# One pool of six PSUM banks, in-place operands counted as inputs, and another order of attention steps in a two-layer encoder trunk

## The chip, the cores and the metric

The kernel runs on one core of a Trainium2 chip. Its engines are TensorE (PE, with weight loads as PEld), VectorE (DVE), ScalarE (ACT), GpSimd (POOL) and SyncE (SP, which issues the DMAs). The metric is device microseconds of one launch. The kernel before has a median of 954.72 us in three runs (953.11 to 955.43).

## The reference

256 tokens of width 1024 pass two layers. Each layer is a half-step SwiGLU block, a mixer, and a second half-step SwiGLU block (width 2816); every block adds to the residual. The mixer of layer 0 is recurrent, that of layer 1 is differential attention whose keys and values are made from the residual between the layers:

```python
x = x + 0.5 * swiglu(rmsnorm(x, g1), wg, wu, wd)
# layer 0
proj = h @ w_in;  gate, rec = split(proj)
rec = causal_depthwise_conv(rec, conv_w, conv_b)          # 4 taps
r, i = sigmoid(rec @ w_a + b_a), sigmoid(rec @ w_x + b_x)  # blocks of 128
a = exp(-8 * r * softplus(-lam))
h_t = a_t * h_{t-1} + sqrt(1 - a_t**2) * i_t * rec_t
x = x + (gelu(gate) * h) @ w_out
# layer 1, 8 heads with two query/key halves of 64 each, chunk-causal mask
q, k = rope(rmsnorm(h @ w_q)), rope(rmsnorm(hkv @ w_k));  v = hkv @ w_v
p = softmax(mask(q @ k.T));  attn = p[0] - lam * p[1]
x = x + (rmsnorm(attn @ v) * (1 - lam0)) @ w_o
x = x + 0.5 * swiglu(rmsnorm(x, g2), wg, wu, wd)
```

Inputs, weights and output are float32.

## The kernel before, in words

Activations lie transposed in SBUF, as eight tiles of 128 features by 256 tokens. Every float32 product is made from three fp32r products: operands are split into a rounded part (`hi`) and a rest (`lo`), and `hi*hi + hi*lo + lo*hi` is summed in PSUM (`mm2` writes the two halves of the activation side by side, 512 columns and then 256; `mm3` issues three matmuls into one sum). Weights come from one array `wts`, laid out by the host in the order in which the steps use them, in pieces of 1 MB; SP loads a piece into `raw`, ACT casts eight 128x128 blocks into `whi` and DVE subtracts to get `wlo` (`split`). So each weight costs PE, ACT and DVE work.

Four stages of feed-forward (`ffn`) surround the two mixers. The recurrent stage (`recurrent`) follows `REC_STEPS`: R0 to R7 are projections of eight feature blocks, each followed by its four-tap convolution on DVE (`taps`: the first tap on ACT, then three in-place `scalar_tensor_tensor`, then a split); L0 to L7 the gate products of those blocks; G the gate projections; D the decay; E the GELU; M the merge; O the output projection. The attention stage follows `ATT_STEPS`: Q, K and V are projections (0: heads 0 to 3, 1: heads 4 to 7; each makes one tile for each of two blocks of 128 tokens, 48 matmuls of 512 columns in all); after Q and K come the norm, the rotation and a transpose (`qk_post`); S0 and S3 are the softmaxes of the first token block for four heads, S1, S2, S4 and S5 those of the second for two heads (`softmax`: scores, on DVE a mask and a maximum, on ACT one exponential for each head and half with a sum, on DVE the combination, on PE a transpose); A0 to A6 multiply with the values and normalise (`av`: its output is squared and scaled on ACT, then transposed on PE); O is the output projection. The letters behind a step say from which PSUM group its tiles come.

PSUM has eight banks. Before, `MB = 4` of them serve tiles named `mm`, `SB = 2` tiles named `sc`, `AB = 2` the tiles `aux` (transposes, norms, the products of A, L0, L1 and L7 of the recurrent stage). A step with tag `m` takes the next free `mm` bank, one with `s` the next free `sc` bank.

The order on each engine is not the order of the code. All calls are recorded (`Recorder.add`, which finds the earlier operations each one depends on from the memory it reads and writes), and `Recorder.plan` lays them out on the five engines: it takes at each step the operation that can start first, with a preference for the one with the longest chain behind it (`tails`), from a duration that `cost` gives. The recorded order of TensorE operations is itself a chain in `tails`, so it acts as their priority. `emit` then issues everything, which is why all instructions carry line 375. In the queues each engine works strictly in that order. `add` distinguishes, for two operations on one engine, a true read after write (`op.raw`: the second waits for the result) from mere order (the second starts when the first has been issued). The inputs are taken as all operands that are not the very object of the output, so an operation that overwrites an operand in place, such as a tap `xcj = rp*w + xcj`, is not counted as reading it.

Of the kernel before, what the change touches and what calls it, by code (L numbers as in the profile page):

```python
# [11 lines left out]
F32 = mybir.dt.float32  # L12
# [6 lines left out]
P = 128  # L19
D = 1024  # L20
KD = 8
T = 256
# [6 lines left out]
SUBLN_EPS = 1e-5  # L29
FG = 2  # L30
REC_STEPS = (
    "W R0s W R1s R2s R3s R4m L0a L1a R5s R6m W L2s L3s R7s G0m D0 L4m L5m L6m L7a G1s E0 E1 G2m E2 "
    "G3s M0 E3 D1 H4a M1 M2 E4 M3 H6m O0 M4 E5 M5 W W O1 E6 M6 E7 O2 O3 M7"
).split()
ATT_STEPS = (
    "Q0mm K0ss K1mm S0mm S1mm Q1ss V0mm A0 S2ms S3ms A2 V1sm S4mm S5mm O0 A4 O1 O2 A6 O3 O4 O5"
).split()
REC_OUT = "0m 1m 23m 45m 67s"
ATT_OUT = "0m 1m 23m 45m 67s"
# [24 lines left out]
DA = 1  # L64
SA = 2
DM = (8, 8, 8, 7)
MB = 4
SB = 2
AB = 2

B_GU = NF * KD * 2
# [24 lines left out]
def is_ap(v):  # L96
    return hasattr(v, "tensor") and hasattr(v, "ap")


def width(v):  # L100
    n = 1
    for _, c in v.ap[1:]:
        n *= c
    return n


def region(v):
    size = mybir.dt.size(v.dtype)
    row = v.ap[0][0]
    lo = v.offset % row if row else v.offset  # L110
    hi = lo + sum(s * (c - 1) for s, c in v.ap[1:]) + 1
    if v.space == bass.MemoryType.PSUM:
        return 0, 1 << 20
    return lo * size, hi * size


def cost(op):
    k, out = op.k, op.outs[0] if op.outs else None
    ins = [v for v in list(op.a) + list(k.values()) if is_ap(v) and not any(v is o for o in op.outs)]
    psum = [v for v in ins if v.space == bass.MemoryType.PSUM]  # L120
    n = width(out) if out is not None else 1
    if op.eng == "tensor":
        if op.fn == "transpose":
            return 109, 220
        m = width(k["rhs"])
        if k["rhs"].dtype == BF16:
            return m / 2.4 + 3, m / 2.4 + 175
        if k["rhs"].dtype == F32R:
            return 0.4508 * m + 2.6, 0.4508 * m + 165
        p = 4 * m / 2.4 + 3 if m > 8 else 222  # L130
        if k["lhsT"].ap[0][1] <= HD:
            p /= 2
        return p, p + 170
    if op.eng == "scalar":
        if op.fn == "preload_act_table":
            return 1294, 1283
        scaled = is_ap(k.get("scale")) or is_ap(k.get("bias"))
        p = n / 1.2 + ((65 + 20 * scaled) if psum else (100 + 85 * scaled))
        lat = n / 1.2 + (172 if psum else 195 + 90 * scaled)
        return (p + 93, lat + 200) if len(op.outs) > 1 else (p, lat)  # L140
    if op.eng == "vector":
        if op.fn in ("reduce_sum", "reduce_max"):
            n = width(ins[0])
        if op.fn == "tensor_copy":
            return n / 1.92 + 67, n / 1.92 + 155
        if op.fn == "memset":
            return n / 0.96 + 10, n / 0.96 + 50
        if op.fn == "tensor_tensor_scan":
            return n * 2 / 0.96 + 55, n * 2 / 0.96 + 140
        rate = 0.96  # L150
        if op.fn == "tensor_scalar" and not psum:
            rate = 1.92
        scalar = op.fn in ("tensor_scalar", "scalar_tensor_tensor") and len(ins) > (1 if op.fn == "tensor_scalar" else 2)
        return n / rate + (125 if scalar else 68), n / rate + (210 if scalar else 153)
    if op.eng == "gpsimd":
        if op.fn == "memset":
            return 30, 100
        if k.get("op") == ALU.pow:
            return 300 + 170 * n, 340 + 170 * n
        return 120 + 2.14 * n, 160 + 2.14 * n  # L160
    return 420, 0


class Recorder:
# [16 lines left out]
    def add(self, eng, fn, a, k):  # L181
        op = Op()
        op.i, op.eng, op.fn, op.a, op.k = len(self.ops), eng, fn, a, k
        op.deps, op.users, op.tiles, op.raw = set(), [], set(), set()
        op.outs = [v for v in ([k["out"]] if "out" in k else list(a[:1])) + [k.get("accum_out")] if is_ap(v)]
        ins = [v for v in list(a) + list(k.values()) if is_ap(v) and not any(v is o for o in op.outs)]
        op.pitch, op.lat = cost(op)
        op.port = False
        op.narrow = eng == "tensor" and fn == "matmul" and k["lhsT"].ap[0][1] <= HD
        if eng in ("vector", "gpsimd"):  # L190
            big = [v for v in ins if v.space != bass.MemoryType.PSUM and width(v) > 1]
            one = fn in ("tensor_scalar", "tensor_copy")
            op.port = len(big) >= (1 if one else 2) and k.get("op") != ALU.pow and fn != "memset"
        for v, w in [(v, False) for v in ins] + [(v, True) for v in op.outs]:
            if v.space == bass.MemoryType.DRAM:
                continue
            name = v.tensor.name
            lo, hi = region(v)
            if name not in self.hist:
                self.hist[name] = []  # L200
                t = v.tensor
                self.tiles[name] = dict(tag=t.tag, bufs=t.tag_meta.bufs, acc=set(), k=self.seen.setdefault(t.tag, 0))
                self.seen[t.tag] += 1
            for j, l, h, ww in self.hist[name]:
                if (w or ww) and l < hi and lo < h:
                    self.depend(op, j)
                    if ww and not w:
                        op.raw.add(j)
            if w:
                self.hist[name] = [x for x in self.hist[name] if not (lo <= x[1] and x[2] <= hi)]  # L210
            self.hist[name].append((op.i, lo, hi, w))
            self.tiles[name]["acc"].add(op.i)
            op.tiles.add(name)
        key = "load" if eng == "sync" and k["out"].space != bass.MemoryType.DRAM else self.key
        if key is not None:
            self.depend(op, self.last.get(key))
            self.last[key] = op.i
        self.ops.append(op)
        return op
# [193 lines left out]
def trunk(ctx: ExitStack, tc, plan, xT, wts, vec, rows, eye, out):  # L413
    nc = Recorder(tc.nc)

    def pool(name, bufs, **kw):
        return Pool(nc, ctx.enter_context(tc.tile_pool(name=name, bufs=bufs, **kw)), bufs, plan and plan[1])
# [5 lines left out]
    wsp = pool("wsp", GB)  # L423
    psm = pool("psm", MB, space=bass.MemoryType.PSUM)
    psa = pool("psa", AB, space=bass.MemoryType.PSUM)
# [62 lines left out]
    def mm2(ps, b, xs, start, stop):  # L488
        wh, wl = wblk(b)
        nc.tensor.matmul(out=ps, lhsT=wh, rhs=xs, start=start, stop=False)  # L490
        nc.tensor.matmul(out=ps[:, 0, :], lhsT=wl, rhs=xs[:, 0, :], start=False, stop=stop)
# [16 lines left out]
    def bank(shape, tag="m"):  # L508
        if tag == "a":
            return psa.tile(shape, F32, name="aux")  # L510
        if tag == "s":
            return psm.tile(shape, F32, name="sc", bufs=SB)
        return psm.tile(shape, F32, name="mm")

    def split_scaled(dst, src, gain):
# [89 lines left out]
    def ffn(i, xs, rb_fn, after, hook=None):  # L605
        rb = None
        hs = []
        o = O_FFN[i]
# [15 lines left out]

        pss = {}
        for f in range(NF):
            pss[f] = ps = [bank([P, 2, T], "mms"[f % 3]) for _ in range(2)]
            if f < FG:
                if f == FG - 1:
                    for k in range(KD):  # L630
                        for ff in range(FG):
                            for j in range(2):
                                mm2(pss[ff][j], o + k * 2 * FG + ff * 2 + j, xs[k], k == 0, k == KD - 1)
            else:
                for k in range(KD):
                    for j in range(2):
                        mm2(ps[j], o + f * 16 + k * 2 + j, xs[k], k == 0, k == KD - 1)
            if f < FG - 1:
                continue
            if f == FG - 1:  # L640
                _, rb = rb_fn()
                for ff in range(FG):
                    finish(ff, pss.pop(ff))
            else:
                finish(f, pss.pop(f))
            if hook and f == 5:
                hook()
        o += B_GU
        for d in range(KD):
            if d < DM[i]:  # L650
                ps = psm.tile([P, 2, T], F32, name="mm")
# [6 lines left out]
            else:  # L658
                ps = psm.tile([P, T], F32, name="mm")
# [89 lines left out]

    xs_mix = new_xs()  # L750
    ffn(0, xs, lambda: rstd("f10"), prep(xs_mix, V_MIX[0]), small)

    def recurrent(xs, rb_fn, after):
# [110 lines left out]
    def after_l0(d):  # L864
        pr1(d)
        split_scaled(xkv[d], x[d], vt[:, V_KV + d:V_KV + d + 1])

    ffn(1, xs_f20, lambda: rstd("f20"), after_l0)

    kvrt = {}  # L870
# [5 lines left out]

    xs_q = new_xs()
    ffn(2, xs_f11, rs_l1, prep(xs_q, V_MIX[1]))

    def attention(xs, rt_q, rt_kv, after):  # L880
# [277 lines left out]
```

## Time and profile before

| | us |
|---|---|
| median of three runs | 954.72 |
| the profiled execution | 954.38 |
| its span, from first to last instruction | 952.6 |
| PE busy | 937.7 |
| DVE busy | 727.9 |
| ACT busy | 582.1 |

Mean granted TensorE clock: 0.995 of full speed. The trace gives for each engine the start and duration of its instructions and, where it was idle before one, what ended the wait. A matmul's duration contains its drain, so durations of neighbours overlap; what one costs is the distance from start to start. In a row of a timeline, x4 stands for four equal instructions in a row, and the bracket at the end holds the idle time before the first of them and what ended it.

### The profile page before, as it was taken

To read this page: it belongs to the slowest core of one execution; us is meant where nothing else is said; L and a number is where in the kernel's file an instruction comes from. 1 tells how busy PE (TensorE), PEld (TensorE's weight loads), DVE (VectorE), ACT (ScalarE), POOL (GpSimd) and SP (SyncE) were. 2 spreads that over 40 slices of the span, in tenths; PEclk is the share of its full clock that TensorE was granted. 3 is DMA by queue.
4 is the path that set the end of the run, shared out by engine and by line. 5 is a ranking of instruction groups with operands and counts; after the bars stand their busy time and mean duration, and the time that the engine had idled before them with its cause. 6 is when DMAs were issued, how large, how long until landed. Compare 5 with 4: busy or idle time off the path is not lost. (4 is left out here: it accounts for less than half of the span.)

```text
span 952.6 us, 14673 instructions
## 1 busy us (share of the span) xinstructions
PE 937.7 (98%) x5586; PEld 828.9 (87%) x5586; DVE 727.9 (76%) x1226; ACT 582.1 (61%) x1039; POOL 36.7 (4%) x42
## 2 busy tenths in 40 slices
PE   8999999999999999999999999999988999999998
PEld 7888888899998888888888888888776988888887
DVE  7998877689988878866788787667985588788751
ACT  7665565569966565656565656545577766656541
POOL 0400000000000000000000000003110000000000
PEclk9999999999999999999999999999999999999999
DMA  8655556543365555555555555555523245555540
GB/s 321 244 206 182 194 199 221 183 172 131 122 231 182 195 201 177 183 208 184 178 182 206 187 182 195 198 177 177 175 91 132 95 175 194 201 177 186 213 161 17
DMA packets 25991, 172.33 MB, mean 181 GB/s; under 512 B 3136, under 2 KB 4288, under 8 KB 5568
## 3 DMA queue, kind: packets, MB, share of 16 engines
q1 hardware_dynamic: 25920, 171.39, 51.5%
q8 instruction: 44, 0.72, 0.3%
q14 instruction: 27, 0.22, 0.1%
HBM read 170.33 MB, written 1.05 MB: 180 GB/s over the span
## 5 line engine op out<-in xcount | busy, mean ns | idle before, releaser
L375 DVE TENSOR_TENSOR wlo<-raw,whi 128x1024 fp32r<-128x1024 f32 (+1 forms) x321 | 390.7, 1221 | 132.4 <-ACT whi L375 131.2
L375 ACT CAST whi<-raw 128x1024 fp32r<-128x1024 f32 (+1 forms) x321 | 335.8, 1047 | 199.3 <-PE mm L375 140.5
L375 PE MATMUL mm<-xs,whi 128*128 128x512 f32 (+1 forms) x1056 | 352.4, 382 | 1.3 <-DVE xs L375 0.9
L375 PE MATMUL mm<-b,whi 128*128 128x512 f32 (+1 forms) x918 | 282.7, 365 | 1.8 <-ACT w L375 1.7
L375 PE MATMUL mm<-xs,wlo 128*128 128x256 f32 x1008 | 281.3, 280 | 0.1
L375 PEld LDWEIGHTS mm<-xs,whi 128*128 128x128 f32 x1056 | 194.5, 188 | 41.5 <-DVE xs L375 1.4
L375 PE MATMUL mm<-b,wlo 128*128 128x256 f32 x800 | 225.0, 282 | 0.0
L375 PEld LDWEIGHTS mm<-b,whi 128*128 128x128 f32 x918 | 165.7, 189 | 30.8 <-ACT w L375 2.3
L375 PEld LDWEIGHTS mm<-xs,wlo 128*128 128x128 f32 x1008 | 190.3, 189 | 0.8 <-DVE wlo L375 0.5
L375 PE MATMUL sc<-xs,whi 128*128 128x512 f32 (+1 forms) x576 | 182.1, 371 | 0.1
L375 PEld LDWEIGHTS mm<-b,wlo 128*128 128x128 f32 x800 | 152.1, 190 | 0.0
L375 PE MATMUL sc<-xs,wlo 128*128 128x256 f32 x512 | 145.1, 283 | 0.0
L375 PEld LDWEIGHTS sc<-xs,whi 128*128 128x128 f32 x576 | 105.0, 191 | 18.7 <-ACT w L375 0.3
L375 ACT ACTIVATE w<-mm 128x256 f32<-128x256 f32 x151 | 57.7, 384 | 77.5 <-PE mm L375 76.3
L375 PEld LDWEIGHTS sc<-xs,wlo 128*128 128x128 f32 x512 | 97.6, 191 | 0.1
L375 DVE TENSOR_TENSOR w<-mm,w 128x256 f32<-128x256 f32 x120 | 49.8, 420 | 17.0 <-ACT w L375 16.9
L375 DVE TENSOR_TENSOR w<-w,rb 128x512 f32<-128x512 f32 x88 | 60.1, 689 | 0.7
L375 DVE TENSOR_TENSOR w<-w,w 128x256 f32<-128x256 f32 (+2 forms) x104 | 45.2, 439 | 0.1
L375 ACT ACTIVATE w<-w 128x256 f32<-128x256 f32 x88 | 36.4, 418 | 9.8 <-DVE w L375 7.4
L375 ACT ACTIVATE w<-sc 128x256 f32<-128x256 f32 x56 | 21.5, 384 | 31.7 <-PE sc L375 31.7
L375 ACT CAST b<-w 128x256 fp32r<-128x256 f32 x88 | 35.4, 406 | 5.6 <-DVE w L375 5.5
L375 DVE TENSOR_TENSOR b<-w,b 128x256 fp32r<-128x256 f32 x88 | 36.5, 418 | 1.9 <-ACT b L375 1.9
(160 smaller groups left out, 686.2 us busy)
## 6 DMA issues: line engine op xcount, KB each, us to landing
raw<-wts SPq DMA_DIRECT2D x159, 1024.0 KB, 4.8
raw<-wts SPq DMA_DIRECT2D x3, 512.0 KB, 6.8
outT<-xa SPq DMA_DIRECT2D x8, 128.0 KB, 2.0
xa<-xT SPq DMA_DIRECT2D x3, 256.0 KB, 6.0
raw<-wts SPq DMA_DIRECT2D x2, 256.0 KB, 3.7
rw<-rows SPq DMA_DIRECT2D x1, 320.0 KB, 5.9
xa<-xT SPq DMA_DIRECT2D x1, 260.0 KB, 3.6
ident<-eye SPq DMA_DIRECT2D x1, 64.0 KB, 9.1
```

The costliest lines, as they stand in the source:

```text
L375: getattr(getattr(self.nc, op.eng), op.fn)(*op.a, **op.k)
```

## The change

Four things change. The two groups `mm` (4 banks) and `sc` (2) become one group of six. `cost` and `add` take their inputs from a new helper, `sources`, which counts an operand that is also the output. The letters `s` vanish from the tables, and `ATT_STEPS` has another order: both K projections directly after Q0 (K1 first), S1 before Q1 and S0 after it, S2 and S3 around the first A2 of the list, A6 before O2. `ATT_STEPS` also orders the weights on the host, so the pieces of K1 and K0 change places.

```diff
 ATT_STEPS = (
-    "Q0mm K0ss K1mm S0mm S1mm Q1ss V0mm A0 S2ms S3ms A2 V1sm S4mm S5mm O0 A4 O1 O2 A6 O3 O4 O5"
+    "Q0mm K1mm K0mm S1mm Q1mm S0mm V0mm A0 S2mm A2 S3mm V1mm S4mm S5mm O0 A4 O1 A6 O2 O3 O4 O5"
 ).split()
...
-MB = 4
-SB = 2
+MB = 6
...
+def sources(a, k):
+    vals = list(a if "out" in k else a[1:]) + [v for n, v in k.items() if n not in ("out", "accum_out")]
+    return [v for v in vals if is_ap(v)]
...
 def cost(op):
     k, out = op.k, op.outs[0] if op.outs else None
-    ins = [v for v in list(op.a) + list(k.values()) if is_ap(v) and not any(v is o for o in op.outs)]
+    ins = sources(op.a, k)
...
-        ins = [v for v in list(a) + list(k.values()) if is_ap(v) and not any(v is o for o in op.outs)]
+        ins = sources(a, k)
         op.pitch, op.lat = cost(op)
...
-        if tag == "s":
-            return psm.tile(shape, F32, name="sc", bufs=SB)
...
-            pss[f] = ps = [bank([P, 2, T], "mms"[f % 3]) for _ in range(2)]
+            pss[f] = ps = [bank([P, 2, T], "m") for _ in range(2)]
```

Since the planner decides, the diff does not show what moves. Three places do. In all of them a number behind a name counts the tiles in recorded order.

PE in attention, from the last matmul of Q1 to the start of V0, before: `mm_1466` and `mm_1467` are the two halves of S0, `mm_1476` and `mm_1477` those of S1, `sc_1526` the second half of S2, `mm_1507` and `mm_1508` the two token blocks of V0.

```order
L375 MATMUL sc_1486<-whi_1490,xs_0_1012 128x512
L375 MATMUL mm_1466<-b_0_1383,b_0_1381 128x128
L375 MATMUL mm_1467<-b_0_1383,b_0_1381 128x128
...
L375 MATMUL mm_1476<-b_0_1383,b_0_1381 128x256
L375 MATMUL mm_1477<-b_0_1383,b_0_1381 128x256
...
L375 MATMUL sc_1526<-b_0_1383,b_0_1381 128x256 x2
L375 MATMUL mm_1507<-whi_1493,xk_644 128x512
...
L375 MATMUL mm_1508<-whi_1493,xk_644 128x512
```

The same place after the change: here `mm_1466` and `mm_1467` are S1, `mm_1498` and `mm_1499` S0, and `aux_1492` is the transpose of the first token block of Q1.

```order
L379 MATMUL mm_1477<-whi_1481,xs_0_1012 128x512
L379 MATMUL mm_1466<-b_0_1383,b_0_1381 128x256
L379 MATMUL mm_1467<-b_0_1383,b_0_1381 128x256
...
L379 MATMUL mm_1498<-b_0_1383,b_0_1381 128x128
L379 MATMUL mm_1499<-b_0_1383,b_0_1381 128x128
...
L379 MATMUL mm_1507<-whi_1484,xk_644 128x512
...
L379 MATMUL mm_1507<-whi_1512,xk_644 128x512
L379 MATMUL aux_1492<-ident_79,w_2_1490 128x128 x4
```

S1 stands before S0, the second half of S2 is gone from here, and V0 starts in one bank alone: nineteen matmuls of its first token block come before the second block takes a bank. By the planner's list of banks V0 took those of S0 before; now its first block takes that of Q1's first block, and its second block that of S1's first half.

ACT between V0 and the transposes inside V1, before: `w_3_1529` and `w_1_1530` are the exponentials of S2, `w_4_1539` and `w_5_1540` those of S3, and the rows with `aux_1519` square (with `oss`) and scale (with `ofr`) the output of A0.

```order
L375 ACTIVATE w_3_1529,sm_1528<-mm_1525,mx_1527,facq_0_1387 128x256 x2
L375 ACTIVATE w_1_1530,sm_1528<-sc_1526,mx_1527,facq_0_1387 128x256 x2
L375 ACTIVATE w_2_1522,oss_1520<-aux_1519,ra_1472 128x128
...
L375 ACTIVATE w_4_1539,sm_1538<-mm_1535,mx_1537,facq_0_1388 128x128 x4
L375 ACTIVATE w_5_1540,sm_1538<-sc_1536,mx_1537,facq_0_1388 128x128 x4
L375 ACTIVATE w_2_1522<-aux_1519,ofr_1523 128x128 x4
```

The same place after the change; S3's exponentials are now `w_5_1545` and `w_2_1546`.

```order
L379 ACTIVATE w_3_1529,sm_1528<-mm_1525,mx_1527,facq_0_1387 128x256
L379 ACTIVATE w_4_1522,oss_1520<-aux_1519,ra_1504 128x128
...
L379 ACTIVATE w_3_1529,sm_1528<-mm_1525,mx_1527,facq_0_1387 128x256
L379 ACTIVATE w_0_1530,sm_1528<-mm_1526,mx_1527,facq_0_1387 128x256 x2
L379 ACTIVATE w_5_1545,sm_1544<-mm_1541,mx_1543,facq_0_1388 128x128 x4
L379 ACTIVATE w_2_1546,sm_1544<-mm_1542,mx_1543,facq_0_1388 128x128 x4
L379 ACTIVATE w_4_1522<-aux_1519,ofr_1523 128x128 x4
```

The same sixteen instructions stand ahead of the four that scale A0's output; only the squares have moved up between those of S2.

PE in the recurrent stage, at L6 (`mm_572`), L7 (`aux_574`) and the gate projection behind them (`sc_576`, now `mm_576`), before:

```order
L375 MATMUL mm_572<-w_4_553,xk_460 128x256 x6
L375 MATMUL aux_574<-w_5_562,xk_460 128x256 x6
L375 MATMUL sc_576<-xs_0_122,whi_554 128x256 x2
L375 MATMUL sc_576<-xs_0_122,wlo_555 128x256
L375 MATMUL sc_576<-xs_0_123,whi_554 128x256 x2
```

and after:

```order
L379 MATMUL mm_572<-w_4_553,xk_460 128x256 x6
L379 MATMUL mm_576<-xs_0_122,whi_554 128x256 x2
...
L379 MATMUL mm_576<-xs_0_123,whi_554 128x256 x2
L379 MATMUL aux_574<-w_5_562,xk_460 128x256
...
L379 MATMUL mm_576<-xs_0_125,whi_554 128x256
L379 MATMUL aux_574<-w_5_562,xk_460 128x256 x5
```

Ten matmuls of the gate projection have moved ahead of most of L7.

## Rows read from the trace of the kernel before

**Rows 1.** Page, part 1: busy time, share of the span, instructions of each engine.
```profile
PE 937.7 (98%) x5586; PEld 828.9 (87%) x5586; DVE 727.9 (76%) x1226; ACT 582.1 (61%) x1039; POOL 36.7 (4%) x42
```

**Rows 2.** Windows by stage: length, busy time by engine, granted clock, DMA share, GB/s.
```profile
205.00:235.00 30.00, 28.34 (x220) 27.73 (x219) 27.94 (x56) 27.23 (x49) 0.00 (x0) 0.94 0.31 106
290.00:640.00 350.00, 350.00 (x2021) 308.49 (x2020) 266.54 (x409) 205.02 (x352) 0.70 (x1) 1.00 0.54 189
...
688.00:708.00 20.00, 17.41 (x93) 13.70 (x92) 17.13 (x46) 14.10 (x36) 3.14 (x2) 0.91 0.26 101
...
729.20:763.80 34.60, 32.84 (x245) 30.88 (x244) 19.53 (x44) 23.81 (x60) 2.01 (x2) 0.95 0.39 137
763.80:945.00 181.20, 180.75 (x1053) 159.47 (x1052) 131.83 (x204) 97.25 (x166) 1.61 (x1) 1.00 0.49 170
```

**Rows 3.** Timeline of PE in attention: start, length, instruction, idle time before.
```profile
672.16 0.63 PE L375 MATMUL aux<-ident,w 128*128 128x128 f32 x4 [0.30 <-DVE w L375]
...
684.44 0.63 PE L375 MATMUL aux<-ident,w 128*128 128x128 f32 x4 [0.30 <-DVE w L375]
...
693.10 0.50 PE L375 MATMUL mm<-whi,xk 128*128 128x512 f32 x1 [2.26 <-ACT w L375]
...
694.86 0.79 PE L375 MATMUL mm<-whi,xk 128*128 128x512 f32 x1 [0.33 <-ACT w L375]
...
718.24 0.58 PE L375 MATMUL aux<-ident,w 128*128 128x128 f32 x2 [1.33 <-ACT w L375]
...
721.16 0.65 PE L375 MATMUL aux<-ident,w 128*128 128x128 f32 x4 [0.23 <-ACT b L375]
...
737.61 0.50 PE L375 MATMUL mm<-b,whi 128*128 128x256 f32 x2 [1.71 <-ACT w L375]
```

**Rows 4.** Timeline of the recurrent stage, at L7: PE, and a weight cast on ACT.
```profile
224.70 0.39 PE L375 MATMUL aux<-w,xk 128*128 128x256 f32 x1 [1.01 <-ACT w L375]
225.60 0.86 PE L375 MATMUL aux<-w,xk 128*128 128x256 f32 x5 [0.52 <-DVE w L375]
...
224.56 1.04 ACT L375 CAST whi<-raw 128x1024 fp32r<-128x1024 f32 x1
```

**Rows 5.** Windows around the four longest stalls of PE; the clock stands third from last.
```profile
223.50:231.00 7.50, 5.97 (x35) 5.58 (x34) 6.19 (x13) 7.35 (x11) 0.00 (x0) 0.77 0.41 133
687.00:699.00 12.00, 9.41 (x52) 6.96 (x51) 10.24 (x33) 9.28 (x29) 0.00 (x0) 0.86 0.25 88
716.00:723.00 7.00, 5.44 (x36) 4.13 (x35) 3.27 (x10) 6.54 (x22) 0.00 (x0) 1.00 0.22 92
733.00:744.00 11.00, 9.29 (x60) 8.42 (x59) 6.04 (x22) 6.85 (x16) 0.00 (x0) 0.84 0.29 97
```

**Rows 6.** Timeline of PE in a projection of 512 columns.
```profile
664.46 0.62 PE L375 MATMUL mm<-whi,xk 128*128 128x512 f32 x2
...
665.14 0.62 PE L375 MATMUL mm<-whi,xk 128*128 128x512 f32 x2
```

**Rows 7.** Timeline of ACT: after Q1, then S2, A0's squares, S3, A0's scaling.
```profile
687.38 0.59 ACT L375 COPY w<-sc 128x512 f32<-128x512 f32 x1 [0.74 <-PE sc L375]
687.87 0.69 ACT L375 ACTIVATE w<-sc,rt_mix 128x512 f32<-128x512 f32 x1
...
710.73 0.56 ACT L375 ACTIVATE w<-mm,mx,facq 128x256 f32<-128x256 f32 x1 [0.85 <-DVE mx L375]
...
712.90 0.37 ACT L375 ACTIVATE w<-aux,ra 128x128 f32<-128x128 f32 x1
...
714.27 0.49 ACT L375 ACTIVATE w<-mm,mx,facq 128x128 f32<-128x128 f32 x1
...
717.75 1.21 ACT L375 ACTIVATE w<-aux,ofr 128x128 f32<-128x128 f32 x4
```

**Rows 8.** Timeline of DVE: six in-place taps of two blocks; two independent combinations.
```profile
200.94 2.96 DVE L375 SCALAR_TENSOR_TENSOR w<-rbuf,vt,w 128x256 f32<-128x256 f32 x6 [0.34 <-ACT w L375]
...
714.78 0.88 DVE L375 SCALAR_TENSOR_TENSOR w<-w,rm,w 128x256 f32<-128x256 f32 x2
```

More of the change, by code (lines that the diff above doesn't have):

```diff
@@ L31 @@
 REC_STEPS = (
-    "W R0s W R1s R2s R3s R4m L0a L1a R5s R6m W L2s L3s R7s G0m D0 L4m L5m L6m L7a G1s E0 E1 G2m E2 "
-    "G3s M0 E3 D1 H4a M1 M2 E4 M3 H6m O0 M4 E5 M5 W W O1 E6 M6 E7 O2 O3 M7"
+    "W R0m W R1m R2m R3m R4m L0a L1a R5m R6m W L2m L3m R7m G0m D0 L4m L5m L6m L7a G1m E0 E1 G2m E2 "
+    "G3m M0 E3 D1 H4a M1 M2 E4 M3 H6m O0 M4 E5 M5 W W O1 E6 M6 E7 O2 O3 M7"
 ).split()
 ATT_STEPS = (
-    "Q0mm K0ss K1mm S0mm S1mm Q1ss V0mm A0 S2ms S3ms A2 V1sm S4mm S5mm O0 A4 O1 O2 A6 O3 O4 O5"
+    "Q0mm K1mm K0mm S1mm Q1mm S0mm V0mm A0 S2mm A2 S3mm V1mm S4mm S5mm O0 A4 O1 A6 O2 O3 O4 O5"
 ).split()
```

## The prediction

> **What bounds the kernel now.** I read the shares of the engines first, then the windows by stage, then the timeline of PE where it stood idle, then ACT and DVE in those places. PE is busy 937.7 us of a span of 952.6 [rows 1], so all its idle time is 14.9 us, 1.6%. The windows say where it is not: between 290 and 640 us PE is busy 350.00 of 350, at full clock, and behind 763.8 it is busy 180.75 of 181.2 [rows 2]. PE's instructions in those feed-forward stages stand in the same order after the change, so nothing is to be had there. What can move is the recurrent mixer (205 to 235: PE 28.34 of 30, DVE 27.94, a clock of 0.94) and attention (clocks of 0.91 and 0.95 in two windows) [rows 2].
>
> In attention PE waits 0.30 + 0.30 for DVE at the transposes of K, 2.26 + 0.33 for ACT at the head of V0, 1.33 + 0.23 at the transposes of A0's output, and 1.71 at O0 [rows 3]: 6.46 us together. At L7 it waits 1.01 and 0.52 [rows 4], 1.53.
>
> To the waits comes the clock. Four windows stand round the long stalls [rows 5]. In three of them PE's clock fell behind the stall to its lower level, 1.2 GHz, for part of the window: 0.77 over 7.5 us, 0.86 over 12, 0.84 over 11. At full clock the work would have been shorter by about the missing share, so these falls cost 7.5 x 0.23 = 1.7, 12 x 0.14 = 1.7 and 11 x 0.16 = 1.8 us. In the fourth, with 1.33 + 0.23 of waits, the clock stayed at 1.00. Waits and falls of both mixers add up to 1.53 + 6.46 + 5.2 = 13.2 us. That is all that a better order can give: 941.2 at best.
>
> **The change part by part.** PE's instructions are the same in number and size, so only waits and clock count. The sum is made on the profiled 954.38 us.
>
> *Head of V0.* Before, V0 takes the banks of S0 and waits until ACT has read them with eight exponentials: 2.26, then 0.33 for the second bank [rows 3]. After, its first token block takes the bank of Q1's first block, which ACT frees with a copy (0.59) and a square (0.69) while PE still has S1 and S0 to do [rows 7]; that wait goes. Its second bank, the first half of S1, is asked for nineteen 512-column matmuls later, 19 x 0.227 = 4.3 us (three in 0.68 us) [rows 6], by which time S1's four exponentials are nearly done. What is late next are the transposes of S1 and S0 inside V0, since both softmaxes now finish under V0 alone. An exponential of 256 columns takes (712.90 - 710.73) / 4 = 0.54, one of 128 columns (717.75 - 714.27) / 8 = 0.435 [rows 7]: S1's four take 2.17, S0's eight 3.48, and before S0's stand copies of Q1 and S1 that PE's transposes have to feed first. Walking PE, DVE and ACT through their new orders with these pitches, I get a wait of about 0.8 at S1's transposes and 0.65 at S0's. Neither value has a row; the bounds are 0 and the old 2.59, and I take the walk's 1.45. Net -1.14. Two waits under 0.9 are shorter than any stall here that was followed by a fall, so its 1.7 goes as well.
>
> *Transposes of A0's output.* They wait for four scalings on ACT. From S2's first exponential to those scalings ACT takes 717.75 - 710.73 = 7.02 us [rows 7], and the same sixteen instructions stand before them after the change. Half of S2 was issued before V0 and now comes after it, so ACT starts some 0.3 later after V0's end (3.0 instead of 2.7) and the first two transposes are ready at 3.0 + 7.02 + 0.6 = 10.6. PE arrives at 1.9 (S2, S3) + 1.5 (A0) + 23 x 0.227 (V1) [rows 6] = 8.6. The wait is 2.0 instead of 1.56: +0.5. Stalls above 1.5 were followed by a fall in three of four places [rows 5], so I book one here: +1.7. Bounds: 0 and 2.2.
>
> *O0.* Its first tile waited 1.71 for S4's exponentials [rows 3]. With six banks S4 and S5 have four of their own before O's, and the wait falls into pieces of about 0.65 in all (by the same walk; bounds 0 and 1.71). -1.06, and the fall of 1.8 that stood behind it goes.
>
> *K's transposes.* They stand about six matmuls of 512 columns later (1.4 us) behind the DVE work that was 0.30 late: -0.60 [rows 3]. Bounds: nothing gained, and 0.60.
>
> *Recurrent stage.* Ten matmuls of the gate projection now stand ahead of most of L7, five of them before its first one. Against that, ACT casts a weight block (1.04, pitch some 0.94) [rows 4] before R7's rounded part, not behind it. The first wait becomes 1.01 + 0.94 - 5 x 0.114 - 0.15 (ACT was idle for the last tap, and the weight cast need not wait for it) = 1.2; 0.114 is half of the 0.227 [rows 6]. The second, 0.52, goes behind the next five matmuls, and with it 0.27 that the lone first matmul (0.39 long) [rows 4] left uncovered. Net 1.2 - 1.53 - 0.27 = -0.6. A stall of 1.2 lies between the one without a fall (1.33) and those with one, so I take half of the fall's 1.7: -0.85. Bounds: the old waits and the whole fall (+1.45 on my sum), or no fall at all (-0.85).
>
> The second half arrives in time only if DVE, which has two more products ahead of R7's rest, saves elsewhere. Six in-place taps took 2.96, 0.49 each; two independent combinations had a pitch of about 0.40 [rows 8]. The new order alternates taps of two blocks, some twelve places at 0.09, so about 1.1 us less against 0.7 more. The Trainium skill (VectorE: DVE Perf Modes, The DRAIN you can't avoid) says that the next operation starts only when the pipe is empty and that leaving out the waits between copies saves nothing; by that, the alternation is worth nothing and the term would be -0.4. The rows show the difference, and I stay with -0.6.
>
> *At nothing:* the K1 and K0 pieces trade places on SP's queue. DMA is busy half of the time and PE does not wait for a load in any row of attention, with pieces several matmul groups ahead; uncovered, a late piece would show as one wait of PE at K1. `cost` is used by the planner alone.
>
> Sum: -1.14 - 1.7 + 0.5 + 1.7 - 1.06 - 1.8 - 0.6 - 0.6 - 0.85 = -5.55, so 948.8. The median of the runs is 0.34 above the profiled execution: 949.2.
>
> **The rivals.** (1) Two clock falls fewer than I booked: none behind A0's output, since 1.56 of waiting there brought none before [rows 5], and none at L7. 949.2 - 1.7 - 0.85 = 946.6. Against it: that wait grows beyond the 1.71 that did bring one. The Trainium skill (TensorE: Matmul & The Clock Gate, What's actually happening) calls the window in which activity is judged free-running, so that the point of change shifts from run to run; by that, whether these two stalls are followed by a fall is a matter of phase, which bears out giving this case a chance of its own.
>
> (2) The wait at V0 only moves. The walk rests on ACT running S1's and S0's exponentials without a gap; if the transposes of both together cost what the banks did (2.59) and the fall of 1.7 follows them, and L7 keeps its fall: 949.2 + 1.14 + 1.7 + 0.85 = 952.9. For it speaks that the number of ACT's instructions is unchanged and ACT is busy 14.10 of 20 us there [rows 2]; against it, that V0's 48 matmuls give it 10.9 us of cover.
>
> (3) Slower: a chain through ACT's in-order queue. S0's eight exponentials stand behind the copy of S1's transposes. If S1's transposes come L later than I walked, S0's exponentials, S0's transposes and V0's end come L later, and so do S3's scores, whose banks are S0's: 2 x L, with falls behind both waits (3.4). 949.2 + 2L + 3.4 passes 954.7 from L = 1.1; at L = 3, S1's full DVE and ACT work again, 958.6.
>
> (4) Counting in-place operands changes the plan and not the chip: recurrent as before, 949.2 + 1.45 = 950.7.
>
> **How the numbers follow.** Forecast 0.45, (1) 0.20, (2) 0.17, (3) 0.08, (4) 0.10. Three per mille, 2.9 us, is what a measurement of this kernel can tell from no change: faster means below 951.9, slower above 957.6. Faster: most of the forecast, all of (1), nearly all of (4), little of (2), 0.70; the same: the rest of these and half of (3), 0.23; slower 0.07. With every bound on the good side (-1.7 behind A0, -1.45 at V0, -0.65 at O0, -0.85 at L7) the time is 944.5, with the bad ones (V0 +2.84, O0 +2.85, L7 +1.45) 956.3. The range is 944.5 to 954.8, which leaves out (3) and the last of the bad corner.
>
> **What would show it.** Right: no wait of 2 us at V0's first matmul; small ones at its transposes for S1 and S0; one of about 2 us at A0's output with a clock below 1.00 behind it; no 1.7 at O0; at L7 one wait near 1.2; feed-forward windows as before. Wrong: V0 with waits of over 1.5 us at one place and a fall of the clock behind it, a longer wait than 2.5 at A0's output, or L7 with its two waits unchanged.

## The result and the profile after

The changed kernel takes 941.62 us (median of 4 runs, 941.29 to 942.00) against 955.08 for the kernel before in the same comparison: a ratio of 0.9862, with a 95% interval from 0.9845 to 0.9879. The forecast of 949.2 had the sign and most of the places right, and less than half of the size; the measured time lies below the range.

The page's first part, of the kernel after; it answers to [rows 1]:

```profile
span 939.9 us, 14667 instructions
...
PE 930.3 (99%) x5586; PEld 824.5 (88%) x5586; DVE 723.9 (77%) x1226; ACT 581.2 (62%) x1039; POOL 31.9 (3%) x42
```

The span is 12.7 us shorter. Idle time of PE went from 14.9 to 939.9 - 930.3 = 9.6 us, 5.3 less. The other 7.4 us left PE's *busy* time, with the same 5586 matmuls. That number is where the forecast went wrong, and the rest of this document follows it.

The windows by stage of the kernel after (length, busy time of PE, PEld, DVE, ACT and POOL, granted clock, DMA share, GB/s), for [rows 2]:

```profile
205.00:235.00 30.00, 29.92 (x249) 29.72 (x249) 28.62 (x61) 27.43 (x48) 0.00 (x0) 1.00 0.33 112
290.00:640.00 350.00, 350.00 (x2018) 308.42 (x2017) 265.60 (x407) 204.68 (x352) 0.70 (x1) 1.00 0.54 190
688.00:708.00 20.00, 19.22 (x112) 15.34 (x111) 17.94 (x54) 17.28 (x55) 5.27 (x3) 1.00 0.34 112
...
729.20:763.80 34.60, 34.59 (x256) 32.48 (x255) 24.80 (x50) 26.23 (x61) 2.01 (x2) 1.00 0.42 146
```

Both mixers now run at a clock of 1.00, where before they had 0.94, 0.91 and 0.95. Feed-forward is what it was. PE's waits of the kernel after, behind the first 20 us, are three (start, length, instruction, idle time before; against [rows 3, 4]):

```profile
697.47 0.30 PE L379 MATMUL aux<-ident,w 128*128 128x128 f32 x1 [0.78 <-DVE w L379]
...
711.15 0.85 PE L379 MATMUL aux<-ident,w 128*128 128x128 f32 x3 [1.75 <-ACT w L379]
...
724.09 0.50 PE L379 MATMUL mm<-b,whi 128*128 128x256 f32 x2 [0.16 <-ACT w L379]
```

They stand at S0's transposes, at A0's, and in O0. The 2.26 at V0's head, the 1.71 at O0 and both waits of L7 are gone. K1, whose weight pieces changed places, has no wait.

Where the time came from is best read by counting PE's matmuls: the stages issue the same numbers, so the start of the n-th one in one kernel can be set against the n-th in the other. A stage's row is by how much that difference grew in it. (Worked out from the starts in the traces of all five kernels; the four in the middle are the experiments below.)

| us against before | only in-place rule | only six banks | both, old order | six banks and new order | all (the change) |
|---|---|---|---|---|---|
| up to the recurrent stage | +0.55 | +0.68 | +0.47 | +0.76 | +1.03 |
| recurrent, to behind L7 | -3.04 | -2.25 | -3.63 | -2.26 | -3.64 |
| from there to Q0 | -0.64 | +0.29 | -0.62 | +0.29 | -0.63 |
| attention | -0.53 | -3.43 | -3.73 | -6.21 | -8.80 |
| behind attention | -0.69 | -0.07 | -0.69 | -0.07 | -0.69 |
| sum | -4.35 | -4.79 | -8.20 | -7.49 | -12.73 |

The first row is start-up: PE's first matmul of layer 0 waits 1.97 us for DVE in the profiled execution after, 0.92 before. The 0.63 of the third row is not safely the change's: a second execution of the kernel before is 0.65 shorter there too. The recurrent output projection lies in that row as well. With six banks and without the in-place rule PE waits there 0.86 us (0.85 with the new order) for DVE, and with the rule it doesn't, which is why the two columns without the rule stand at +0.29.

### The profile page after: what moved, and what is told of

Same layout as the page of the kernel before. It is cut to its first block, busy times and chain, and to the rows that moved or that the text cites. A ratio compares the mean times of both kernels' runs of the same rounds, so it can differ in the third digit from the quotient of the medians.

```text
span 939.9 us, 14667 instructions
## 1 busy us (share of the span) xinstructions
PE 930.3 (99%) x5586; PEld 824.5 (88%) x5586; DVE 723.9 (77%) x1226; ACT 581.2 (62%) x1039; POOL 31.9 (3%) x42
## 4 chain that ended last, share of the span: by engine, by line
PE 95%; ACT 3%; DVE 1%; DMA 0%; issue 0%; SPq 0%; ACTq 0%
PE mm L379 92%; PE aux L379 3%; ACT w L379 2%; ACT b L379 1%; DMA xa<-xT 0%; ACT whi L379 0%; DVE wlo L379 0%; ACT L379 0%; DVE mx L379 0%; DVE w L379 0%; ACT xs L379 0%; DVE xs L379 0%; DVE xa L379 0%; SPq L379 0%; DVE mm L379 0%
## 5 line engine op out<-in xcount | busy, mean ns | idle before, releaser
L379 PE MATMUL mm<-xs,whi 128*128 128x512 f32 (+1 forms) x1632 | 531.6, 378 | 2.0 <-DVE xs L379 2.0
L379 PE MATMUL mm<-xs,wlo 128*128 128x256 f32 x1520 | 426.2, 281 | 0.0
L379 PEld LDWEIGHTS mm<-xs,whi 128*128 128x128 f32 x1632 | 298.9, 188 | 60.3 <-DVE xs L379 2.3
L379 PEld LDWEIGHTS mm<-xs,wlo 128*128 128x128 f32 x1520 | 287.9, 190 | 0.5
L379 ACT ACTIVATE w<-mm 128x256 f32<-128x256 f32 x207 | 79.5, 385 | 115.4 <-PE mm L379 110.8
L379 DVE TENSOR_TENSOR w<-mm,w 128x256 f32<-128x256 f32 x176 | 73.5, 421 | 27.1 <-ACT w L379 27.0
L379 PE MATMUL mm<-whi,xk 128*128 128x512 f32 x128 | 42.1, 400 | 0.0
L379 PEld LDWEIGHTS mm<-whi,xk 128*128 128x128 f32 x128 | 24.0, 188 | 4.7
L379 PE MATMUL mm<-wlo,xk 128*128 128x512 f32 x64 | 25.2, 394 | 0.0
L379 ACT ACTIVATE xs<-xa,vt 128x256 fp32r<-128x256 f32 x40 | 19.7, 504 | 8.9 <-DVE xa L379 8.7
```

The costliest lines, as they stand in the source:

```text
L379: getattr(getattr(self.nc, op.eng), op.fn)(*op.a, **op.k)
```

## The experiments

**Which part does it.** Four kernels with parts of the change. Their edits, from the kernel before and from the kernel after:

```diff
# only_sources: before, with sources and these lines
+    ins = sources(op.a, k)          # in cost
+        ins = sources(a, k)         # in add
# no_order: after, with the old order of attention
+    "Q0mm K0mm K1mm S0mm S1mm Q1mm V0mm A0 S2mm S3mm A2 V1mm S4mm S5mm O0 A4 O1 O2 A6 O3 O4 O5"
# no_sources: after, with this line in cost and in add again
+    ins = [v for v in list(op.a) + list(k.values()) if is_ap(v) and not any(v is o for o in op.outs)]
# only_pool: no_sources and no_order together
```

> The kernel before with in-place operands counted as inputs and nothing else (four and two banks, old attention order). Theory A (the recurrent stage's gain comes from the planner alternating the in-place taps): no wait over 0.4 us at L7 and no fall of the clock there, the recurrent stage 3 to 4 us shorter, attention within 1 us of before with its waits of 2.3 at V0 and 1.7 at O0; 950 to 951.5 us. Theory B (it comes from the six banks): recurrent as before, 954 to 955.

Measured: 950.45, ratio 0.9925 (0.9900 to 0.9949). L7 has one wait, of 0.54 where 0.4 was the bound, and no fall; attention keeps 2.24 at V0 and 1.71 at O0. Theory A, but for the 0.14.

> Six banks in one group and nothing else (old attention order, in-place operands not counted). Theory A: L7 keeps its two waits of together 1.5 and the fall behind them; some of attention's waits move; 950 to 954. Theory B: recurrent 3 to 4 us shorter, no wait at L7; 948 to 951.

Measured: 949.50, ratio 0.9919 (0.9893 to 0.9945). A miss for both. The timeline of PE in this kernel at L7, and the window round it:

```profile
224.93 0.38 PE L379 MATMUL aux<-w,xk 128*128 128x256 f32 x1 [1.00 <-ACT w L379]
225.50 0.87 PE L379 MATMUL aux<-w,xk 128*128 128x256 f32 x5 [0.19 <-DVE w L379]
```

```profile
223.50:231.00 7.50, 6.32 (x51) 5.91 (x50) 5.67 (x12) 7.36 (x11) 0.00 (x0) 1.00 0.27 90
```

The first wait is the old one, the second fell from 0.52 to 0.19, and no fall follows (1.00, where [rows 5] have 0.77). That is most of the 2.25: 0.33 and the fall's 1.7. So the recurrent gain is not the in-place rule's alone: in these executions either part was enough to save the fall, and the rule takes most of the waits as well.

> The changed kernel with the old order of attention steps (six banks, in-place operands counted). If attention's gain of 8.8 us is the order's, V0 or the step after it still has a wait of over 1.5 us with a fall of the clock behind it, and the time is 946 to 950. If it is the banks', attention is as short as in the changed kernel and the time is 941 to 943.

Measured: 948.58, ratio 0.9908 (0.9879 to 0.9937). The time is in the range for the order, but the wait isn't at V0 or behind it, as expected: with six banks the old order moves it forward into Q1. PE in this kernel, there and at A0's transposes:

```profile
677.24 0.79 PE L379 MATMUL mm<-whi,xs 128*128 128x512 f32 x1 [3.50 <-ACT w L379]
...
714.69 0.33 PE L379 MATMUL aux<-ident,w 128*128 128x128 f32 x1 [2.04 <-ACT w L379]
...
728.45 0.50 PE L379 MATMUL mm<-b,whi 128*128 128x256 f32 x2 [0.25 <-ACT w L379]
```

In this plan Q1 takes the banks of S0 and waits 3.50 us for ACT's first exponentials of S0, with a fall. The banks in the old order do what was forecast at O0 (1.71 became 0.25 here and 0.24 with the banks alone), and the new order takes away the wait that the banks only moved. The new order with the old groups of four and two banks was not run.

> The changed kernel without counting in-place operands (six banks, new order). Theory A: attention as short as in the changed kernel (within 1 us), recurrent as before with waits of 1.5 at L7 and a fall of the clock; 945 to 946.5. Theory B (banks make the recurrent gain): 941.5 to 942.5.

Measured: 946.72, ratio 0.9886 (0.9862 to 0.9911). The recurrent stage is as with the banks alone, not as before, and the time is 0.2 above Theory A's range. Attention is 2.6 us longer than in the changed kernel, more than the 1 us expected: 1.7 of that is a fall behind A0's transposes, whose wait is 1.94 here and 1.75 there.

**What sets a fall of the clock.** The next runs repeat kernels to see whether falls come again at the same places.

> The changed kernel once more. If a fall of the clock behind a wait were set by the wait's length alone, the 1.75 us at A0's transposes would again be followed by none. If it also depends on when the wait comes, another execution may show a fall there (1.7 us longer) and the times spread by about that: 941 to 943.5.

Measured: 944.62 (943.10 to 945.83), ratio 0.9874 (0.9846 to 0.9903); in the profile 0.80, 1.76 and 0.17, no fall. The times lie above the range all the same. The profiled execution lost 2.7 of its 2.8 us on the earlier one ahead of the recurrent stage, with no wait and a clock of 1.00: from 80 to 110 us PE issued 172 matmuls in it, 175 in the earlier one.

> The kernel before once more, for its falls of the clock alone. Theory P (a matter of the place: what PE does round a wait decides): falls again behind the waits at L7, V0 and O0, none behind the 1.33 + 0.23 at A0's transposes. Theory F (a matter of phase, which differs between executions): another set of falls, at least one of the four places answers differently.

Measured: 954.55. The same windows as [rows 5], moved by 0.7 us in the first, in this execution:

```profile
224.20:231.70 7.50, 5.98 (x35) 5.58 (x34) 6.19 (x13) 7.35 (x10) 0.00 (x0) 0.77 0.41 137
687.00:699.00 12.00, 9.41 (x51) 6.94 (x50) 10.22 (x33) 9.18 (x29) 0.00 (x0) 0.86 0.25 88
716.00:723.00 7.00, 5.44 (x35) 4.14 (x34) 3.17 (x11) 6.65 (x22) 0.00 (x0) 1.00 0.25 103
733.00:744.00 11.00, 9.29 (x60) 8.42 (x59) 5.92 (x22) 6.85 (x16) 0.00 (x0) 0.84 0.29 97
```

All four clocks are those of [rows 5].

> The changed kernel without counting in-place operands once more. Its profiled execution had a wait of 1.94 us at A0's transposes with a fall of the clock behind it, and 1.00 + 0.19 at L7 with none. Theory P: the same again. Theory F: no fall behind the 1.94, or one at L7.

Measured: 946.68; 1.94 with a fall again, 0.98 + 0.18 with none again. In three kernels traced twice the same places had a fall. That is less than Theory P says, for two reasons.

The first is that the moment was not the same. In the two executions of this kernel the 1.94 ends at 714.29 and at 714.22. The granted clock is still 1.00 for 1.2 us behind it in the first and down to 0.50 within 0.2 us in the second, as a window of each shows:

```profile
714.30:715.50 1.20, 1.20 (x8) 0.95 (x9) 1.20 (x7) 1.20 (x4) 0.00 (x0) 1.00 0.00 0
```

```profile
714.40:715.60 1.20, 1.20 (x5) 0.94 (x5) 1.18 (x7) 1.20 (x4) 0.00 (x0) 0.50 0.00 0
```

The second is that not every execution has the falls. In the kept traces three falls go with a mean granted clock of 0.995 (the kernel before, twice), two with 0.996 (only_sources, only_pool), one with 0.998 (no_order, no_sources twice, and the kernel after, at start-up), none with 0.999 or 1.000. Of the 31 executions of the kernel before that were run beside these experiments, nine show 0.994 or 0.995, eighteen 0.996, two 0.998 and two 1.000; of the six of no_sources two show 1.000. So some executions miss falls that others of the same kernel have, and 1.7 us between two single profiles can be the execution's and not the kernel's. What decides is open. The wait's length alone doesn't tell, as the window round A0's transposes shows in three kernels, of which the first is the one without counting in-place operands (wait 1.94), the second the one with banks alone (2.04), the third the one with the old order (2.04):

```profile
712.00:719.00 7.00, 5.06 (x21) 3.88 (x20) 4.50 (x11) 5.96 (x18) 0.00 (x0) 0.76 0.26 108
```

```profile
714.00:721.00 7.00, 4.96 (x21) 4.13 (x21) 4.16 (x11) 6.04 (x19) 0.00 (x0) 0.76 0.23 98
```

```profile
712.00:719.00 7.00, 4.96 (x27) 3.64 (x26) 4.42 (x13) 6.84 (x21) 0.00 (x0) 1.00 0.30 128
```

**Which half of the in-place rule.**

```diff
# sources_add: after, with this line in cost alone
-    ins = sources(op.a, k)
+    ins = [v for v in list(op.a) + list(k.values()) if is_ap(v) and not any(v is o for o in op.outs)]
```

> The changed kernel with in-place operands counted when dependences are recorded, but not in the planner's durations. Theory A1 (the gain at L7 is from the dependences: an in-place tap is planned to wait for the tap before it, so taps of two blocks alternate): L7 without waits over 0.2, as fast as the changed kernel, 941 to 942.5. Theory A2 (it is from the longer planned duration of an in-place tap): L7 waits 1.0 to 1.2 as without the change, 944 to 946.

Measured: 946.57, ratio 0.9900 (0.9871 to 0.9929). L7 waits 0.23, where 0.2 was the bound, and the recurrent stage is 0.5 us longer than in the changed kernel: A1, the dependences do most of it. The time is a miss: with other durations the plan of attention changes too and O0 waits 2.13.

**What is left, and why.** The 1.75 at A0's transposes was the one forecast wait that stayed. Two kernels attack it, one from the queue's side and one from the plan's:

```diff
# scale_dve: after, in av
-                nc.scalar.activation(o[:, i, :], po[:, i, :], AF.Copy, scale=fr[:, i:i + 1])
+                if h0 == 0:
+                    nc.vector.tensor_scalar(o[:, i, :], po[:, i, :], fr[:, i:i + 1], None, op0=ALU.mult)
+                else:
+                    nc.scalar.activation(o[:, i, :], po[:, i, :], AF.Copy, scale=fr[:, i:i + 1])
# accum_cost: after, in cost
-        return (p + 93, lat + 200) if len(op.outs) > 1 else (p, lat)
+        return (p + 243, lat + 350) if len(op.outs) > 1 else (p, lat)
# acc_dve: both, the first with h0 in (0, 6)
```

> The changed kernel with the four scalings of A0's output on DVE, out of ACT's queue. If the 1.75 us at A0's transposes is ACT's in-order queue (S3's eight exponentials of 0.435 stand ahead of the scalings, 3.5 us), the wait falls below 0.3 and the time to 939 to 940.5. Rival: the transposes wait for the norm's chain (square, pow, product) or DVE becomes late for S2's and S3's combinations, and the wait stays or moves to A2: 941 to 943.

Measured: 940.59, ratio 0.9837 (0.9809 to 0.9865). The wait at A0's transposes is 0.17; PE's timeline in this kernel shows what took part of its place:

```profile
710.69 0.50 PE L379 MATMUL aux<-ident,w 128*128 128x128 f32 x2 [0.17 <-DVE w L379]
...
714.28 1.60 PE L379 MATMUL aux<-b,b 128*128 128x128 f32 x12 [1.22 <-ACT b L379]
```

The products of the next A step now wait 1.22 for ACT, which copies their operand behind S3's exponentials and a weight cast. Each theory had a half right.

> The changed kernel with 150 ns more in the planner for an activation that also sums (measured 0.435 and 0.54 us, planned 0.285 and 0.39). The plan then puts A0's scalings ahead of six of S3's eight exponentials. If the wait at A0's transposes comes from the planner's too short exponentials, it falls from 1.75 to below 0.6, and the time to 939.5 to 941. Rival: what is taken from A0 is paid at A4 or A6, whose chains now start later: 941 to 944.

Measured: 939.18, ratio 0.9821 (0.9792 to 0.9850), and 939.16, 0.9836 (0.9816 to 0.9857), when repeated. No wait at all up to the end of V1, and one behind it. PE and ACT in the first of these runs:

```profile
734.92 1.10 PE L379 MATMUL aux<-ident,w 128*128 128x128 f32 x4 [1.29 <-ACT w L379]
```

```profile
733.56 1.04 ACT L379 CAST whi<-raw 128x1024 fp32r<-128x1024 f32 x1 [1.66 <-PE mm L379]
734.51 1.13 ACT L379 ACTIVATE w<-aux,ofr 128x128 f32<-128x128 f32 x4
```

The scalings stand behind a weight cast that itself waited 1.66 for PE: the in-order queue again, with another instruction at its head.

> The changed kernel with the longer planned duration once more, beside the run above on the same chip: 938.3 to 940, with one wait of 1.2 to 1.4 us in attention and no fall.

Measured: the 939.16 given above, with one wait of 1.29 and no fall.

> The changed kernel with 150 ns more in the planner for an activation that also sums, and the scalings of A0's and A6's outputs on DVE. If the 1.29 us that the longer planned duration alone left near the output projection comes from the scalings standing in ACT's queue, it goes and the time is 1 to 1.7 us below that of the kernel with the longer planned duration alone: 937.5 to 938.5. Rival: DVE becomes late for S2 and S3 as it did with the scalings on DVE alone (1.22 at A2): 939 to 940.

Measured: 936.24 (935.83 to 937.78), ratio 0.9802 (0.9784 to 0.9819): an interval wholly below the change's, and 2.9 us less than the longer durations alone in the same comparison. The time is below the range, and the gain is more than the 1 to 1.7 us expected. Between the two profiles lie 3.2 us: 1.9 at the place of the 1.29, where the transposes behind the wait also stood 0.26 apart, 0.4 at start-up, and some 0.9 that was not separated. Behind the first 20 us PE has no wait of 0.15 us or more. Its windows over the recurrent stage and the whole of attention, and its page:

```profile
205.00:235.00 30.00, 29.93 (x250) 29.72 (x249) 28.63 (x60) 27.41 (x48) 0.00 (x0) 1.00 0.35 119
...
680.00:763.00 83.00, 82.92 (x566) 73.60 (x565) 69.34 (x170) 67.71 (x171) 8.90 (x7) 1.00 0.42 148
```

```profile
span 934.1 us, 14668 instructions
...
PE 927.4 (99%) x5586; PEld 823.2 (88%) x5586; DVE 725.5 (78%) x1234; ACT 578.8 (62%) x1031; POOL 33.1 (4%) x42
```

## Why the prediction was wrong, step by step

The sum was -5.55 and the profiles differ by -12.73. The terms missed by -2.2 (recurrent), -1.5 (head of V0), -1.8 (A0's transposes), -1.6 (O0) and +0.2 (K's transposes); what had no term is -0.7 behind attention, -0.6 between the mixers and +1.0 at start-up. Together that is the -7.2 between the two.

**The ceiling failed.** The working put all idle time and all falls of the mixers at 13.2 us and "941.2 at best". The last kernel is 952.6 - 934.1 = 18.5 us below before in span, with a start-up 0.45 us longer; 3.6 of it lie in the recurrent stage and 14.0 in attention, 17.6 in all (it also moves eight scalings from ACT to DVE, so not all of this is order). An idle time in the timeline begins where the last matmul's *modelled end* lies, not where the next one could have been issued. The rows at L7 show it: from 224.70 to 225.60 are 0.90 us for one matmul whose neighbours stand 0.12 apart, so it cost 0.78, and the bracket says 0.52; the rest counts as busy. PE in the kernel after, at A0's transposes:

```profile
709.02 0.39 PE L379 MATMUL mm<-wlo,xk 128*128 128x512 f32 x1
711.15 0.85 PE L379 MATMUL aux<-ident,w 128*128 128x128 f32 x3 [1.75 <-ACT w L379]
```

Here 2.13 from start to start less a pitch of 0.23 is 1.90 for a bracket of 1.75. Each wait that goes gives back 0.15 to 0.3 more than its bracket. In the sum of the change: idle -5.3, three falls less one at start-up -3.4, and the remaining -4.0 of the 12.7 was in busy time that no bracket showed. The waits that went explain about half of that; the rest, smaller gaps between matmuls, was not separated. The Trainium skill (Perfetto Trace Analysis, Identifying the Most-Contended Engine) says that the busy share of matmuls is not a good measure of how close a kernel is to its roofline, because they are pipelined. The 7.4 us of busy time that went here, with the same matmuls, agree.

**The recurrent term: -1.45 booked, -3.64 measured.** The step that failed is "the first wait becomes 1.01 + 0.94 - 5 x 0.114 - 0.15 = 1.2". It kept the times of ACT's instructions and added the weight cast ahead of the cast that makes R7's rounded part. That cast in the kernel before, then both in the kernel after:

```profile
224.25 0.41 ACT L375 CAST w<-w 128x256 fp32r<-128x256 f32 x1
```

```profile
223.56 1.04 ACT L379 CAST whi<-raw 128x1024 fp32r<-128x1024 f32 x1
224.50 0.40 ACT L379 CAST w<-w 128x256 fp32r<-128x256 f32 x1
```

Against [rows 4] the weight cast starts 1.0 us earlier on the axis, and this kernel entered the stage 1.0 us late: 2.0 earlier. R7's cast behind it starts 0.25 later on the axis, so 0.8 earlier by the same count, where the sum had it 0.8 later (0.94 - 0.15). ACT's own instructions there wait for what DVE evicts and sums: between 213 and 221 us it waited for DVE 0.48 + 0.23 + 0.31 + 0.46 us before, and 0.16 after. So DVE's gain reaches ACT, and the cast that was to cost 0.94 was out of the way. DVE's gain is as forecast. Its six taps of two blocks, alternating in the kernel after, against 2.96 in [rows 8]:

```profile
201.97 2.56 DVE L379 SCALAR_TENSOR_TENSOR w<-rbuf,vt,w 128x256 f32<-128x256 f32 x6 [0.34 <-ACT w L379]
```

By the Trainium skill (VectorE: DVE Perf Modes, The DRAIN you can't avoid) alternation should have gained nothing; 0.40 us less for the same six instructions decides against it for operations that read what the one before wrote. (The same section adds that a next op that is not held starts earlier; no run here shows whether that is the case.) With no wait left, the half fall of 0.85 that the sum kept did not come either. It was booked on a slip: a stall of 1.2 does not lie between the 1.33 without a fall and those with one, but below both.

**Head of V0: -2.84 booked, -4.33 measured.** From the first score to A0's first product are 710.96 - 687.96 = 23.00 before and 702.54 - 684.30 = 18.24 after, 4.76 less; but the stretch before holds four matmuls of S4 (0.43 us) that stand behind it after. PE in the kernel before, then after:

```profile
687.96 2.03 PE L375 MATMUL mm<-b,b 64*128 64x128 f32 x24
...
710.96 1.60 PE L375 MATMUL aux<-b,b 128*128 128x128 f32 x12
```

```profile
684.30 2.03 PE L379 MATMUL mm<-b,b 64*128 64x256 f32 x24
...
702.54 1.60 PE L379 MATMUL aux<-b,b 128*128 128x128 f32 x12
```

The mechanism held: no wait for a bank, the fall gone, a wait for S0's combination in its place, 0.78 for the 0.65 walked. S1's 0.8 did not come. That is 0.67 of the 1.5 missed; the other 0.8 stands in no bracket.

**A0's transposes: +2.2 booked, about +0.4 measured** (from A0's first product to O0). The wait was forecast as 2.0 and is 1.75; the fall that "three of four" made likely did not come in either trace. A frequency over four places of one execution was no rule: lengths don't decide, and executions differ. Rival (1) had this right, and its 946.6 still carried the waits at V0 and L7. How far that was luck is open: the nine executions of the changed kernel show clocks of 0.998 to 1.000, at most one fall in any. The scalings' place in ACT's queue as the cause is confirmed by the two kernels that move them.

**O0: -2.86 booked, about -4.4 measured** from there to the end of attention: the wait is 0.16 instead of 0.65, the fall is gone, and about 1 us stands in no bracket. Six banks alone bring this wait to 0.24, but they don't ensure it: the kernel that counts in-place operands only in the dependences also has six banks, and its plan waits 2.13 there.

**K's transposes: -0.60 booked, -0.42 measured.** The wait is gone as forecast.

**What had no term:** the transition behind attention, -0.69. It goes with the in-place rule (first, third and last column of the table, not the second and fourth): PE's 0.45 wait for DVE at the norm's sums is in the kernels without the rule. "Nothing is to be had" held for the feed-forward matmuls, not for the seam.

Rivals (2) to (4) fell: no wait of the old size moved under V0, no chain through ACT's queue grew, and the in-place rule does change the chip's time (-3.0 in the recurrent stage by itself).

## What to carry to other kernels

Price a wait of a pipelined engine from start to start against the neighbours' pitch, not by the idle time in the bracket, and price what it does to the clock separately, from more than one execution; the ceiling from "idle" alone was a quarter too low here. When one engine of a chain gets faster, move the next engines' times too before adding a new instruction to their queues. A planner is worth its durations: 150 ns more for activations that sum, read from the trace, gave 2.4 us against the changed kernel's first median and 5.4 against the one beside it.

## What was not expected of the hardware

Falls of PE's clock cost about 1.7 us each. In three kernels traced twice they came at the same places (three of three in the kernel before, one of one without the in-place rule, none behind the start-up in the kernel after), but the mean clocks show other executions of the same kernels with fewer or none. The Trainium skill (TensorE: Matmul & The Clock Gate, What's actually happening) says that the moment of change varies from run to run; the two traces without the in-place rule agree, with a fall over 1.2 us behind the end of a wait in one and within 0.2 us in the other. Waits of 1.71, 1.94 and 2.04 had a fall, others of 1.75, 1.92, 2.04 and 2.13 had none; what tells them apart stays open. And one execution issued matmuls some 2% slower for its first stage at a granted clock of 1.00 and without waits (172 against 175 in 30 us); no run here explains it.
